# The warm-up products of an encoder layer's opening read a constant, and are 16 instead of 14

## The chip, the cores and the metric

The kernel runs on one core of a Trainium2 chip. The time is that of the device in microseconds (us), from the program's start to its end; a kernel is run several times, and the median counts. A profile shows one further execution: when every instruction began on each engine, how long it took and what ended the idle time before it. The engines are PE (TensorE, matrix products; PEld is its loading of weights), DVE (VectorE), ACT (ScalarE), POOL (GpSimd) and SP (SyncE, which here sends off transfers). "PEq", "SPq" are the instruction sequencers of an engine. Times in the profile count from the first instruction of the execution.

## The reference

One layer of a streaming encoder in float32, for a sequence of 256 frames of width 2048.

```python
h = rms_norm(x, attn_norm)
x = x + hybrid_mixer(h, w_in, b_forget, q_norm, k_norm, out_norm_fox, out_norm_sb, w_out)
h = rms_norm(x, ffn_norm)
x = x + conv_ffn(h, w_up, conv_w, conv_b, w_down)
```

`hybrid_mixer` multiplies h by `w_in` (2048 x 6152), runs eight heads of forgetting attention and eight heads of stick-breaking attention, normalises the two groups apart, and multiplies by `w_out` (2048 x 2048). `conv_ffn` multiplies by `w_up` (2048 x 11264), applies a causal convolution of width 3 over time, gates one half with the SiLU of the other, and multiplies by `w_down` (5632 x 2048).

## The kernel before

Every product of the reference is made of three products of halves. A float32 weight is loaded (`load`, L197, tile `w_raw`), rounded on ScalarE to a coarser type (`w_hi`, L207), and VectorE makes the rest (`w_lo` = raw - hi, L208). TensorE then adds hi x hi, lo x hi and hi x lo in an accumulator (`in_three`, L221, with the tokens as rows; `from_features`, L249, with the features as rows). Activations are split in the same way: `transposed_split` (L133) transposes four blocks of x on TensorE (`ps_x`, L138), and writes the high part on ScalarE (L143) and the low part on VectorE (L146) into `hT`.

The stages, in the program's order:

- **Opening** (L385 to L474). x, the gains and the first weights of `w_in` are loaded in small pieces. While they travel, `keep_busy` (L379) gives TensorE products whose result `idle` nobody reads: 14 before the gains are transposed (`columns`, L126), and 4 more after the first four transposes of x. Their operand is `zeros`, a tile of 128 x 256 bf16 in the pool `at`, written by VectorE (L371). Then the first piece of weights is split, and the first products into `acc` run (L428).
- **Projections and heads** (L481 to L772): the rest of `w_in`, then the sixteen heads.
- **Output projection** (L781 to L807): for each of two groups of heads and each of four blocks c of 512 columns, `acc` is formed with `w_out` (L229), and VectorE adds it to x (L803). In the second group, ScalarE sums the squares of the new x (`junk`, L155), and the transposes of the new x for the FFN wait for a later step (`next_rows`, L776).
- **Factors of the tokens** (`token_factors`, L157): the sums of squares are reduced (L161), and a reciprocal root is taken: two steps on ScalarE (L112, L113), the others on VectorE (L111 to L117); two diagonal tiles `dg` follow (L166).
- **FFN** (L814 to the end): a list of steps. Each has a load, sent off six steps ahead, a split, two steps ahead, and its products; the first column block of `w_up` is `pu` (L254 high, L260 low), in two pieces of 8 x 128 rows.

Tiles live in pools, stacked in memory in the order in which they are opened. The attention stage opens `at` (L289), `tmp`, `wraw` (three buffers of 8192 bytes in each partition), `whi` and `wlo` (two each), and closes them at its end; the FFN opens its own `wlo2`, `whi2` (three each), `wraw2` (four) and `wsum` in the memory that has come free (L814 to L817). The scheduler makes the first instruction that writes to a pool wait for the last readers of what lay in that memory before. In the opening and the FFN the order on each engine is as written; from the end of the opening to the FFN only TensorE's is, and the scheduler chooses the others' by priority and by what it expects to be free.

Of the kernel before, what the change touches and what calls it, by code (L numbers as in the profile page):

```python
# [14 lines left out]
P = 128  # L15
D = 2048
S = 256
# [28 lines left out]
def hybrid_layer(  # L46
# [19 lines left out]
    nc = tc.nc  # L66
    act, dve = nc.scalar, nc.vector
# [10 lines left out]
    def f32(t):  # L78
        return t.bitcast(F32)
# [10 lines left out]
    def load_x(k, n):  # L90
        nc.sync.dma_start(x2[:, :, k * P : (k + n) * P], xp[:, :, k * P : (k + n) * P])
# [34 lines left out]
    def columns(dst, rows, n):  # L126
        pp = psb.tile([P, 512], F32, name="pp", tag="t")
        nc.tensor.transpose(pp[:, :n], rows, ident[:n, :n])
        dve.tensor_copy(dst, pp[:, :n])
# [3 lines left out]
    def transposed_split(k, g, n=2):  # L133

        ps = psb.tile([P, 2, S], F32, name="ps_x", tag="t")
        for j in range(n):
            for t in range(NT):
                nc.tensor.transpose(  # L138
                    ps[:, j, t * P : (t + 1) * P], xt[t][:, (k + j) * P : (k + j + 1) * P], ident
                )  # L140
        for j in range(n):
            i = k + j
            act.activation(hT[:, i, 0, :], ps[:, j, :], AF.Identity, scale=g[:, i : i + 1])  # L143
        for j in range(n):
            i = k + j
            dve.scalar_tensor_tensor(  # L146
                hT[:, i, 1, :], ps[:, j, :], g[:, i : i + 1], f32(hT[:, i, 0, :]),
                op0=ALU.mult, op1=ALU.subtract,
            )

    def sums_of_squares(ss, c, tiles=range(NT)):

        for t in tiles:
            junk = late.tile([P, 512], F32, name="junk", tag="raw", bufs=4)
            act.activation(junk, xt[t][:, c * 512 : (c + 1) * 512], AF.Square, accum_out=ss[:, t, c : c + 1])  # L155
# [62 lines left out]
    def rows_of(w, k0, n, c0, cols):  # L218
        return w[k0 * P : (k0 + n) * P, c0 : c0 + cols].rearrange("(k p) c -> p k c", p=P)
# [14 lines left out]
    def of_half(h, part, t):  # L234
        return h[:, part, t * P : (t + 1) * P]
# [51 lines left out]
    with ExitStack() as actx:  # L287

        at = actx.enter_context(tc.tile_pool(name="at", bufs=1))  # L289
# [77 lines left out]

        zeros = at.tile([P, S], mybir.dt.bfloat16, name="zeros")  # L370
        dve.memset(zeros, 0.0)  # L371
        nc.gpsimd.memset(ident, 0.0)
        nc.gpsimd.affine_select(
            ident, ident, pattern=[[-1, P]], base=0, channel_multiplier=1,
# [2 lines left out]
        idle = pss.tile([P, S], F32, name="idle", tag="s")  # L377

        def keep_busy(n):  # L379
            for _ in range(n):  # L380
                nc.tensor.matmul(idle, zeros[:, :P], zeros, start=True, stop=True)

        ss1 = const.tile([P, NT, 4], F32, name="ss1")

        def opening():  # L385

            acc = psa.tile([P, NT, 512], F32, name="acc", tag="acc")
            pairs = [[(0, 1), (1, 1)]] + [[(0, 2)]] * 7
            raws, parts = [], []

            def load_w(c, which=None, queue=nc.sync):

                if c == len(raws):
                    raw = wraw.tile([P, 2048], F32, name="w_raw", tag="w_raw")
                    raws.extend([raw[:, :1024], raw[:, 1024:]])
                for i, n in [(which, 1)] if which is not None else [(0, 2)]:
                    queue.dma_start(
                        raws[c][:, i * 512 : (i + n) * 512].rearrange("p (a b) -> p a b", a=n),
                        rows_of(wi, 2 * c + i, n, 0, 512),
                    )  # L400

            def split_w(c):
                hi = whi.tile([P, 2048], F32R, name="w_hi", tag="w_hi")
                lo = wlo.tile([P, 2048], F32R, name="w_lo", tag="w_lo")
                parts.append([t[:, :1024].rearrange("p (a b) -> p a b", a=2) for t in (hi, lo)])
                for i, n in pairs[c]:
                    cols = slice(i * 512, (i + n) * 512)
                    if c == i == 0:
                        dve.tensor_copy(hi[:, cols], raws[c][:, cols])
                        for k in range(2):  # L410
                            transposed_split(k, ga, 1)
                    elif c == 1:
                        for j in range(2):
                            half = slice(512 * j, 512 * (j + 1))
                            dve.tensor_copy(hi[:, half], raws[c][:, half])
                        transposed_split(2, ga)
                    else:
                        act.copy(hi[:, cols], raws[c][:, cols])
                    dve.tensor_tensor(
                        lo[:, cols], raws[c][:, cols], f32(hi[:, cols]), op=ALU.subtract  # L420
                    )

            def multiply(c, i, n, high):
                hi, lo = (p[:, i : i + n] for p in parts[c])
                order = [(j, l, hi) for j in range(n) for l in range(2)] if high else [(j, 0, lo) for j in range(n)]
                for m, (j, l, r) in enumerate(order):
                    for t in range(NT):
                        nc.tensor.matmul(  # L428
                            acc[:, t, :], of_half(hT[:, 2 * c + i + j], l, t), r[:, j, :],
                            start=high and c == i == m == 0, stop=not high and c == 7 and m == n - 1,  # L430
                        )

            load_x(0, 2)
            nc.scalar.dma_start(prow[:KT, :], attn_norm[0].rearrange("(n p) -> n p", p=P))
            act.preload_act_table_set("natural_log_exp_and_others")
            load_w(0, 0)
            load_w(0, 1, nc.scalar)
            load_x(2, 2)
            load_w(1, 0, nc.scalar)
            load_w(1, 1)  # L440
            load_x(4, 2)
            load_w(2)
            load_x(6, 2)
            load_w(3)
            load_x(8, 4)
            load_w(4)
            load_x(12, 4)
            load_w(5)
            keep_busy(14)
            columns(ga, prow[:KT, :], KT)  # L450
            split_w(0)
            keep_busy(4)

            def behind(c):
                if c:
                    transposed_split(2 * c + 2, ga)
                split_w(c + 1)

            multiply(0, 0, 1, True)
            multiply(0, 1, 1, True)  # L460
            behind(0)
            sums_of_squares(ss1, 0, [0])
            multiply(0, 0, 1, False)
            multiply(0, 1, 1, False)
            for c in range(1, 8):
                if c < 7:
                    behind(c)
                sums_of_squares(ss1, c // 2, [c % 2])
                if c == 2:
                    load_w(6)  # L470
                    load_w(7)
                multiply(c, 0, 2, True)
                multiply(c, 0, 2, False)
            return acc  # L474

        with tc.high_priority(offset=AHEAD), tc.manual_schedule(
            engines={mybir.EngineType.PE, mybir.EngineType.DVE, mybir.EngineType.Activation, mybir.EngineType.SP}
        ):
            acc_q0 = opening()
# [301 lines left out]
        for group in range(2):  # L781
# [3 lines left out]
            for c in range(4):  # L785
# [7 lines left out]
                if c == 0:  # L793
                    pg = psb.tile([P, NT], F32, name="pg", tag="t")
                    for t in range(NT):
                        nc.tensor.matmul(
                            pg[:, t : t + 1], ssq[group][:, t * P : (t + 1) * P], ones[:, 0:1],
                            start=t == 0, stop=t == NT - 1,
# [376 lines left out]
```

## Time and profile before

| What | us |
|---|---|
| median of three runs (lowest to highest) | 1103.35 (1103.25 to 1103.62) |
| the profiled execution's own time | 1103.81 |
| its span, from the first to the last instruction | 1102.0 |
| TensorE busy in the span | 1096.5 |
| VectorE busy | 877.7 |
| ScalarE busy | 701.9 |
| GpSimd busy | 44.4 |

The span is the time that the engines' instructions cover; the execution's own time has some start and end beside it (1.8 us here). The mean granted clock of TensorE over the span is 1.000 of full speed. The profile is read by groups (the page), by what each engine waited for, by a timeline of one stretch, and by the chain of waits, which is followed back from the last instruction. A row such as "6.02 0.43 DVE L409 CAST ... [1.56 <-DMA ...]" says: began at 6.02 us, took 0.43 us, on VectorE, line 409; VectorE had been idle for 1.56 us, until a transfer landed.

### The profile page before, as it was taken

What the parts mean: (1) busy time and instruction counts of PE and PEld (TensorE: products, weight loads), DVE (VectorE), ACT (ScalarE), POOL (GpSimd) and SP (SyncE); (2) the same over time, 40 slices, a digit from 0 to 9 for tenths busy, and PEclk for the clock granted to TensorE, in tenths of its full rate; (3) what the DMA queues carried; (4) which work ended last, traced back from release to release, by engine and by line L of the source; (5) the groups of instructions that cost most, each with busy time, mean ns of one, the idle gap of its engine ahead of it and who ended that gap; (6) DMA issues with size and microseconds to landing.
All of it is one profiled execution on the core that took longest, in us unless ns stands there. A gap on an engine that the chain in (4) does not pass through costs nothing.

```text
span 1102.0 us, 14826 instructions
## 1 busy us (share of the span) xinstructions
PE 1096.5 (99%) x5868; PEld 951.2 (86%) x5868; DVE 877.7 (80%) x941; ACT 701.9 (64%) x879; POOL 44.4 (4%) x46
## 2 busy tenths in 40 slices
PE   9999999999999999999999999999999999999998
PEld 7998888888888888888888888888888888888887
DVE  5655777975775677689889988889798889889896
ACT  6544556664653566677767776767676777677753
POOL 0000000000000000000000010100000010100010
PEclk9999999999999999999999999999999999999999
DMA  8776654576545396558989597986979689997985
GB/s 288 171 244 230 188 156 153 153 231 197 184 161 186 112 317 196 181 191 209 288 223 312 191 234 264 261 269 177 315 209 303 217 218 282 241 266 198 322 208 177
DMA packets 179407, 245.89 MB, mean 223 GB/s; under 512 B 4432, under 2 KB 119018, under 8 KB 179082
## 3 DMA queue, kind: packets, MB, share of 16 engines
q1 hardware_dynamic: 162458, 209.67, 58.6%
q0 software_dynamic: 16560, 34.75, 16.8%
q8 instruction: 46, 0.75, 0.3%
q10 hardware_dynamic: 320, 0.53, 0.1%
q14 instruction: 23, 0.19, 0.0%
HBM read 242.82 MB, written 2.11 MB: 222 GB/s over the span
## 4 chain that ended last, share of the span: by engine, by line
PE 99%; DMA 0%; DVE 0%; SPq 0%; issue 0%
PE pu L254 34%; PE acc L229 22%; PE pu L260 18%; PE bank_a L229 10%; PE bank_b L229 5%; PE bank_c L229 2%; PE acc L428 2%; PE acc L1053 1%; PE ps_x L138 1%; PE ps_o L593 1%; PE bank_a L1053 1%; PE ps_p L607 0%; DMA w_raw<-in_w_in_dram 0%; PE ps_o L594 0%; PE ps_h L307 0%; PE ps_s L522 0%
## 5 line engine op out<-in xcount | busy, mean ns | idle before, releaser
L208 DVE TENSOR_TENSOR w_lo<-w_raw,w_hi 128x2048 fp32r<-128x2048 f32 (+1 forms) x196 | 439.6, 2246 | 129.5 <-ACT w_hi L207 128.6
L207 ACT CAST w_hi<-w_raw 128x2048 fp32r<-128x2048 f32 (+1 forms) x196 | 367.3, 1877 | 235.9 <-PE acc L229 66.6
L254 PE MATMUL pu<-hT,w_hi 128*128 128x512 f32 x1664 | 394.0, 390 | 0.0
L254 PEld LDWEIGHTS pu<-hT,w_hi 128*128 128x128 f32 x1664 | 310.3, 188 | 63.2
L260 PEld LDWEIGHTS pu<-hT,w_lo 128*128 128x128 f32 x1664 | 211.9, 191 | 7.0
L260 PE MATMUL pu<-hT,w_lo 128*128 128x256 f32 x1664 | 215.1, 283 | 0.0
L229 PE MATMUL acc<-w_hi,hT 128*128 128x512 f32 (+1 forms) x576 | 124.5, 368 | 0.0
L229 PEld LDWEIGHTS acc<-w_hi,hT 128*128 128x128 f32 x576 | 101.5, 188 | 14.3
L207 ACT CAST w_hi<-w_sum 128x2048 fp32r<-128x2048 f32 x30 | 57.3, 1909 | 44.2 <-PE pu L254 36.6
L208 DVE TENSOR_TENSOR w_lo<-w_sum,w_hi 128x2048 fp32r<-128x2048 f32 x30 | 68.7, 2290 | 20.8 <-ACT w_hi L207 20.7
L870 ACT ACTIVATE tap<-up,ccol 128x256 f32<-128x256 f32 x176 | 74.6, 495 | 0.0
L229 PE MATMUL acc<-w_lo,hT 128*128 128x512 f32 (+1 forms) x288 | 64.6, 366 | 0.0
L229 PEld LDWEIGHTS acc<-w_lo,hT 128*128 128x128 f32 x288 | 51.6, 188 | 7.5
L975 POOL DMA_DIRECT2D w_sum<-in_w_down_dram x20 | 25.7, 1284 | 797.7 <-DVE w_lo L208 786.1
L229 PE MATMUL acc<-w_hi,oT 128*128 128x512 f32 x192 | 46.0, 392 | 0.0
L229 PEld LDWEIGHTS acc<-w_hi,oT 128*128 128x128 f32 x192 | 35.7, 188 | 7.3
L229 PE MATMUL bank_a<-w_hi,g 128*128 128x512 f32 x160 | 40.0, 392 | 0.0
L229 PE MATMUL bank_b<-w_hi,s 128*128 128x512 f32 x160 | 40.0, 392 | 0.0
L229 PE MATMUL bank_a<-w_hi,s 128*128 128x512 f32 x160 | 40.0, 392 | 0.0
L229 PEld LDWEIGHTS bank_b<-w_hi,s 128*128 128x128 f32 x160 | 28.9, 189 | 5.2
L229 PEld LDWEIGHTS bank_a<-w_hi,g 128*128 128x128 f32 x160 | 28.8, 189 | 5.3
L229 PEld LDWEIGHTS bank_a<-w_hi,s 128*128 128x128 f32 x160 | 28.9, 189 | 5.2
(211 smaller groups left out, 1068.7 us busy)
## 6 DMA issues: line engine op xcount, KB each, us to landing
w_raw<-in_w_up_dram SPq DMA_DIRECT2D x88, 1024.0 KB, 7.5
w_raw<-in_w_down_dram SPq DMA_DIRECT2D x44, 1024.0 KB, 6.4
w_raw<-in_w_in_dram SPq DMA_DIRECT2D x36, 1024.0 KB, 5.4
w_sum<-in_w_down_dram POOLq DMA_DIRECT2D x20, 1024.0 KB, 9.9
w_raw<-in_w_out_dram SPq DMA_DIRECT2D x16, 1024.0 KB, 5.1
w_raw<-in_w_down_dram POOLq DMA_DIRECT2D x10, 1024.0 KB, 14.9
w_raw<-in_w_in_dram SPq DMA_DIRECT2D x12, 688.0 KB, 4.2
w_raw<-in_w_in_dram SPq DMA_DIRECT2D x6, 512.0 KB, 6.8
```

The lines of the kernel that those rows point to most:

```text
L138: nc.tensor.transpose(ps[:, j, t * P : (t + 1) * P], xt[t][:, (k + j) * P : (k + j + 1) * P], ident)
L207: act.copy(hi[:, :n], raw[:, :n])
L208: dve.tensor_tensor(lo[:, :n], raw[:, :n], f32(hi[:, :n]), op=ALU.subtract)
L229: nc.tensor.matmul(o, lhs(i, l, t), r[:, i, :], start=starts and j == 0, stop=stops and j == 3 * n - 1, skip_group_check=more,)
L254: nc.tensor.matmul(acc[:, j, :], hi[:, i, j * P : (j + 1) * P], hT[:, k].rearrange("p a b -> p (a b)"), start=k == 0, stop=low_first and k ...
L260: nc.tensor.matmul(acc[:, j, S:], lo[:, i, j * P : (j + 1) * P], hT[:, k, 0, :], start=False, stop=not low_first and k == KT - 1,)
L428: nc.tensor.matmul(acc[:, t, :], of_half(hT[:, 2 * c + i + j], l, t), r[:, j, :], start=high and c == i == m == 0, stop=not high and c == ...
L593: nc.tensor.matmul(po, v[j][:, hs], wp[:, k], start=i == 0, stop=False)
L870: act.activation(taps[w][:, j, :], u[:, j, w : w + S], AF.Copy, scale=ccol[:, w, f : f + 1])
L975: nc.gpsimd.dma_start(mem[into][:, : nk * 512].rearrange("p (a b) -> p a b", a=nk), src, accum_op=ALU.add)
L1053: nc.tensor.matmul(o, of_half(g, l, t), r[:, i, c0 : c0 + cols], start=kh == 0 and j == 0, stop=kh == n - 1 and j == 11,)
```

## The change

The tile `zeros` and its memset go. `keep_busy` reads `some`, a view of a constant that the program's preamble writes on GpSimd before any kernel instruction (one bf16 1.0 in each partition, read again and again), and the first call makes 16 products.

```diff
-        zeros = at.tile([P, S], mybir.dt.bfloat16, name="zeros")
-        dve.memset(zeros, 0.0)
+        some = nc.const_aps.tensor(1.0, [P, S], mybir.dt.bfloat16)
...
         def keep_busy(n):
             for _ in range(n):
-                nc.tensor.matmul(idle, zeros[:, :P], zeros, start=True, stop=True)
+                nc.tensor.matmul(idle, some[:, :P], some, start=True, stop=True)
...
-            keep_busy(14)
+            keep_busy(16)
```

The pool `at` is 512 bytes smaller in each partition by this, and the scheduler's order differs from before at three places. Behind the change the lines of the kernel have numbers smaller by one.

VectorE at the start of the program, before and after; what an instruction waits for stands in brackets:

```order
L1170 UNCONDITIONAL_BRANCH [waits barrier_Pool_Activation_PE_DVE_SP_release]
L371 MEMSET zeros 128x128
L129 COPY ga<-pp 128x16 [waits PE_49]
L409 COPY w_hi<-w_raw 128x512 [waits DMAHW2_49]
L146 TENSOR_SCALAR hT<-ps_x,ga,hT 128x256 [waits Activation_49] x2
```

```order
L1169 UNCONDITIONAL_BRANCH [waits barrier_Pool_Activation_PE_DVE_SP_release]
L825 MEMSET up_3577 128x2x2
L825 MEMSET up_3578 128x2x2
L129 COPY ga<-pp 128x16 [waits PE_49]
L408 COPY w_hi<-w_raw 128x512 [waits DMAHW2_49]
```

The memset of `zeros` is gone, and two small memsets of the FFN (`up`, before at the border of the stages) stand in its place.

SP at the border between the output projection and the FFN, as a difference (`DMAHW` and `DMASW` are queues of transfers, the other names engines):

```order
 L200 DMA w_raw<-in_w_out_dram 128x4x512 [waits DMAHW5_49,DVE_49]
-L200 DMA w_raw<-in_w_up_dram 128x8x256 [waits DMAHW6_49,DMAHW0_49,DMAHW7_49,DMASW3_49,DVE_49]
+L200 DMA w_raw<-in_w_up_dram 128x8x256 [waits DMAHW0_49,DMAHW6_49,DMASW3_49,DMAHW7_49,DVE_49,PE_49]
 L200 DMA w_raw<-in_w_up_dram 128x8x256 x3
 L200 DMA w_raw<-in_w_up_dram 128x8x256 [waits DMAHW1_49,DVE_49]
 L200 DMA w_raw<-in_w_up_dram 128x8x256 [waits DMAHW2_49,DVE_49]
```

The first load of `w_up` has a wait for PE that it did not have; the three behind it have none of their own, as before.

ScalarE at the same border, before and after (`w_hi` casts of FFN weights, L207; squares, L155; reciprocal root, L112 and L113; `hT`, L143, the last quarter of x):

```order
L143 ACTIVATE hT<-ps_x,pcol 128x256 [waits PE_49]
L143 ACTIVATE hT<-ps_x,pcol 128x256
L207 COPY w_hi<-w_raw 128x2048 [waits DMASW4_49,DMASW5_49,DMASW2_49,DMAHW1_49,Activation_49,Pool_49]
L207 COPY w_hi<-w_raw 128x2048 [waits DMAHW2_49]
L155 ACTIVATE junk,ss_2828<-x_2945 128x512 [waits DVE_49] x2
L207 COPY w_hi<-w_raw 128x2048 [waits DMAHW3_49]
L112 ACTIVATE rs_y<-rs_a 128x2 [waits DVE_49]
L113 ACTIVATE rs_y<-rs_y 128x2 [waits Activation_49]
```

```order
L143 ACTIVATE hT<-ps_x,pcol 128x256 [waits PE_49]
L143 ACTIVATE hT<-ps_x,pcol 128x256
L155 ACTIVATE junk,ss_2828<-x_2945 128x512 [waits DVE_49,Activation_49] x2
L112 ACTIVATE rs_y<-rs_a 128x2 [waits DVE_49]
L113 ACTIVATE rs_y<-rs_y 128x2 [waits Activation_49]
L207 COPY w_hi<-w_raw 128x2048 [waits DMASW4_49,DMASW5_49,DMASW2_49,DMAHW1_49,PE_49,Pool_49]
L207 COPY w_hi<-w_raw 128x2048 [waits DMAHW2_49]
L207 COPY w_hi<-w_raw 128x2048 [waits DMAHW3_49]
```

The three casts have moved behind the squares and the reciprocal root, and the first of them waits for PE. On VectorE the three `w_lo` of these weights have moved in the same way, behind the reciprocal root and the two `dg`. TensorE's order is the same but for the two added products and the second call of `columns`, which stands two products earlier.

## The prediction

> **What bounds the kernel now.** I read first the busy shares and the chain that ended last (page, parts 1 and 4), then everything that TensorE waited for, then the two places where the order of instructions changes: the opening and the border between attention and the feed-forward part (FFN).
>
> ```profile
> PE 1096.5 (99%) x5868; PEld 951.2 (86%) x5868; DVE 877.7 (80%) x941; ACT 701.9 (64%) x879; POOL 44.4 (4%) x46
> PE 99%; DMA 0%; DVE 0%; SPq 0%; issue 0%
> PE idle L381 <- DVE zeros L371: 1.1, 1, 1.1
> PE acc L428 <- DVE w_hi L409: 1.1, 1, 1.1
> PE ps_x L138 <- DMA x<-in_x_dram: 0.2, 1, 0.2
> ```
>
> TensorE sets the end: 1096.5 of the span of 1102.0 us. The last three rows are its whole list of waits (engine, line, releaser: us, times, longest), and all three lie in the opening. So two things follow. A faster opening can return at most 1.1 + 1.1 + 0.2 = 2.4 us. And after it TensorE has no waiting left that could swallow a delay: whatever holds it at any later place is added to the end one for one.
>
> The timeline of the opening (start, duration, engine, line; in brackets the idle time before and its releaser), and one row of the chain of waits (the DMA):
>
> ```profile
> 0.83 0.17 DVE L371 MEMSET zeros<- 128x128 uint32 x1 [0.83 <-PEq L1160]
> 1.06 3.04 PE L381 MATMUL idle<-zeros 128*128 128x256 bf16 x14 [1.06 <-DVE zeros L371]
> 1.23 4.77 DMA w_raw<-in_w_in_dram
> 4.03 0.22 PE L128 MATMUL pp<-cs,prow 16*128 16x16 f32 x1
> 4.29 0.17 DVE L129 COPY ga<-pp 128x16 f32<-128x16 f32 x1 [3.29 <-PE pp L128]
> 4.45 0.66 PE L138 MATMUL ps_x<-cs,x 128*128 128x128 f32 x4 [0.20 <-DMA x<-in_x_dram]
> 4.93 0.84 ACT L143 ACTIVATE hT<-ps_x,ga 128x256 fp32r<-128x256 f32 x2 [2.42 <-PE ps_x L138]
> 6.02 0.43 DVE L409 CAST w_hi<-w_raw 128x512 fp32r<-128x512 f32 x1 [1.56 <-DMA w_raw<-in_w_in_dram]
> 6.59 2.06 PE L428 MATMUL acc<-w_hi,hT 128*128 128x512 f32 x8 [1.05 <-DVE w_hi L409]
> ```
>
> The first real products start at 6.59 because the first weights land at 1.23 + 4.77 = 6.00. Of what the change touches there, nothing sends that transfer off earlier.
>
> The timeline at the border, and six rows of the chain of waits (the last six; start, duration, what):
>
> ```profile
> 383.96 2.28 DVE L208 TENSOR_TENSOR w_lo<-w_raw,w_hi 128x2048 fp32r<-128x2048 f32 x1
> 386.28 13.29 SPq L200 DMA_DIRECT2D w_raw<-in_w_up_dram  x6
> 389.33 3.89 PE L229 MATMUL acc<-w_hi,hT 128*128 128x512 f32 x16
> 391.42 1.91 ACT L207 CAST w_hi<-w_raw 128x2048 fp32r<-128x2048 f32 x1 [0.67 <-DMA w_raw<-in_w_up_dram]
> 393.36 2.29 DVE L208 TENSOR_TENSOR w_lo<-w_raw,w_hi 128x2048 fp32r<-128x2048 f32 x1 [1.65 <-ACT w_hi L207]
> 394.34 1.92 ACT L207 CAST w_hi<-w_raw 128x2048 fp32r<-128x2048 f32 x1 [1.02 <-DMA w_raw<-in_w_up_dram]
> 395.57 1.40 DVE L803 SCALAR_TENSOR_TENSOR x<-acc,rg,x 128x512 f32<-128x512 f32 x2
> 397.54 0.19 ACT L155 ACTIVATION_READ_ACCUMULATOR junk<-x 128x1 f32 x1
> 399.09 0.15 DVE L161 TENSOR_REDUCE ssum<-ss 128x2 f32<-128x8 f32 x1
> 399.71 0.20 ACT L113 ACTIVATE rs_y<-rs_y 128x2 f32<-128x2 f32 x1
> 389.58 5.46 PE acc L229 x24
> 395.03 1.81 PE pu L254 x8
> 396.85 0.95 PE pu L260 x8
> 397.80 1.84 PE pu L254 x8
> 399.64 0.95 PE pu L260 x8
> 400.59 0.88 PE ps_x L138 x8
> ```
>
> Here the first FFN weights are asked for at 386.28, the moment the last w_lo of the attention stage is made (383.96 + 2.28 = 386.24), are split at 391.42 to 393.33, and so are ready 1.7 us before TensorE leaves the last attention product at 395.03. The border is seamless, by a margin of only 1.7 us.
>
> **The change, part by part.**
>
> *The opening.* The wait for the memset goes: TensorE can begin at about 0.85, when VectorE could begin its memset, and not at 1.06. Two products more, at 3.04 / 14 = 0.217 us each, make 16 x 0.217 = 3.47 us and end near 4.32, against 1.06 + 3.04 = 4.10 now. The transposition of the gains behind them (L128, 4.03) comes some 0.2 later, ga some 0.2 later, the four transposes (4.45) and hT (4.93 to 5.77) at most 0.3 later, 6.07. VectorE uses hT only after its cast of the weights, at 6.02 + 0.43 = 6.45. So 0.4 us of cover is left, under the transfer that lands at 6.00: cost and gain 0. Without that cover it would cost 0.3. The two small memsets of `up` that VectorE now does first take the place of the memset of zeros, in front of 3.29 us of idle time (row of 4.29): 0. The transposition of the parameters (L128, second call) goes two products earlier in TensorE's order and the product gq one place up on VectorE: no work is added, 0.
>
> *The border: the load.* The tile zeros took 512 bytes in each partition. Without it every tile of the attention stage that lies behind it moves down by 512 bytes. The FFN's four raw buffers end at byte 154,656 of a partition; the attention stage's w_hi buffers began at 154,912 and now begin at 154,400. The two overlap by 256 bytes, and the order of SP shows what comes of it: the first load of w_up now waits for PE too. The value it waits for is that of the sixteenth product with the last w_hi of the attention stage, which ends at 389.33 + 3.89 = 393.22 and not 386.24. All later loads on SP are queued behind it. From issue to cast the first load took 391.42 - 386.28 = 5.14 us. That puts the cast at 393.25 + 5.14 = 398.4.
>
> *The border: the order on ScalarE and VectorE.* The same overlap puts ScalarE's casts of the first three FFN weights behind the squares (L155) and the two steps of the reciprocal root (L112, L113), which need the last attention product. When would ScalarE be free? The product ends at 395.04; VectorE's two additions take 1.40 (row of 395.57), to 396.5; the last square's accumulator is read 397.73 - 396.97 = 0.76 after them, 397.2; from the reduction to the end of L113 it takes 399.91 - 399.09 = 0.82: 398.1. This is 0.3 before the load lands, so of the two causes the load decides, and the order alone would give a cast at 398.1 even with the old load. Either suffices for nearly the whole stall.
>
> *The sum.* Cast 398.4 + 1.91 = 400.3. TensorE begins 0.14 later, as it did after the cast at 6.45 (6.59 - 6.45): 400.4. It has stood since 395.04: 5.4 us. Its first eight products end 1.81 later, at 402.2; the next eight need w_lo, 2.29 after the cast, 402.6, and the same 0.1 to begin: 0.5 us more. Then the weights are ahead again: the second load is cast 394.34 - 391.42 = 2.9 after the first, at 401.3, its w_lo is ready at 401.3 + 1.92 + 2.29 = 405.5, and TensorE asks for it after its transposes, at 400.59 + 0.88 + 5.9 = 407.4. The transposes themselves now stand behind a wait for eight products; their order is unchanged. Total 5.4 + 0.5 = 5.9, and with a tenth for the first product's slow start 6.0 us. The profiled execution took 1103.81 us around its span of 1102.0; the span becomes 1108.0. The median of the runs, 1103.35, becomes 1109.4. Bounds of this sum: if transfers after an idle queue land faster, ScalarE's order still holds the cast to 398.1, so 5.6 at least less 0.3 for the starts: 5.3. If the first load needs half a microsecond longer, 6.5.
>
> **The rivals.**
>
> *The clock of TensorE falls in the gap.* The new gap of 5.4 us is longer than any in this trace after the start (1.05 us is the longest). The opening shows what a product costs at first: 0.217 us for 256 columns, against 0.95 / 8 = 0.119 in the row of 396.85, and this for less than 4.95 - 1.06 = 3.9 us. If it were so again, up to 3.9 us at half pace lose 1.9 us, of which 0.4 hide under the wait for w_lo: 0 to 1.5 more, 1109.7 to 1110.9. For it: the gap's length. Against: no row shows how long a gap it takes.
> The Trainium skill, "TensorE: Matmul & The Clock Gate", Part 1, has the clock halved after a whole idle window of about 3.4 us, the windows running free of the kernel; by that rule a gap of 5.4 us holds a whole window in some runs and not in others, which speaks against this change beyond the stall itself; no row of this trace can show it at the border.
>
> *The FFN stays starved.* The loads behind the first are late as well, and if the second landed over 1.9 us (407.4 - 405.5) later than reckoned, TensorE would stop again: 1 to 3 us more, 1110.9 to 1112.4. Against it is the row of the border by slices of 0.8 us:
>
> ```profile
> GB/s 0 0 0 0 0 0 0 0 0 111 360 385 379 348 349 347 348 349 347 349 347 348 349 348 347 349 356 337 346 351 348 346 289 250 335 348 348 348 348 348
> ```
>
> At 350 GB/s a load of 1.05 MB takes 3.0 us, and TensorE needs 1.81 + 0.95 + 1.84 + 0.95 = 5.6 us for each: it catches up 2.6 us with every load.
>
> *Not slower: the opening pays and the border does not.* The border costs nothing if TensorE's last attention products run ahead of the load's wait, which takes two things: a wait that is over by 386.3, and casts that do not sit behind the squares. Then only the opening counts, between 0 and its 2.4 us: 1101.0 to 1103.4. It decides if both orders are harmless; the 1.7 us of margin against 7.0 us of delay (393.22 - 386.24) leave little room.
>
> *It does what it says and no more* (the wait for the memset is gone, the rest hidden): 1103.3, by the same two conditions.
>
> **How the numbers follow.** The stall at full clock has 0.50 and gives 1109.4 (its own range 1108.7 to 1109.9); the fallen clock 0.33; starvation 0.11; the opening paying 0.03; no effect 0.03. The range 1108.3 to 1111.5 holds the first, all of the second, and a third of the third case, with a little below for shorter starts. Within 0.2% means within 2.2 us, about what a measurement can tell: faster 0.03, same 0.03, slower 0.94.
>
> **What would show it.** In the profile after: TensorE's list of waits has a new row, pu (L254) waiting for ScalarE's w_hi, about 5.4 us once, and one for w_lo (L260) of about 0.5; the first SP row of w_up stands near 393.2 and not 386.3; ScalarE's first FFN cast begins at 398 to 399, behind L113; the opening still has its first real product at 6.6. Products of 512 columns at 0.43 us right after the gap would show the fallen clock. The prediction is wrong if the first w_up load is issued by 387, if the cast starts before 396, or if the gap is there and the end is not later by it.

## The result and the profile after

The changed kernel takes 1110.56 us (median of six runs, 1110.18 to 1111.87), the kernel before 1103.3: a ratio of 1.0067, with a 95% interval of 1.0054 to 1.008. It is 7.3 us slower, by an edit that was made 390 us ahead of the place where the time is lost. The profiled execution took 1110.36, its span is 1108.6. Of all runs below one is left out, an execution of the kernel with 224 unused bytes (e4) that took 1566.71 us at a mean clock of 0.654.

TensorE's list of waits (engine, line, releaser: us in total, times, longest) now has these three rows:

```profile
PE pu L254 <- ACT w_hi L207: 5.3, 1, 5.3
PE idle L380 <- PEq L1159: 0.8, 1, 0.8
PE acc L427 <- DVE w_hi L408: 0.6, 1, 0.6
```

The opening waits for 1.4 us and no longer for 2.4. A new wait of 5.3 us stands at the first product of `pu`, and the mean granted clock over the span is 0.998, not 1.000.

The opening in the timeline after:

```profile
0.78 3.33 PE L380 MATMUL idle<-const-bfloat16-1.0 128*128 128x256 bf16 x16 [0.78 <-PEq L1159]
4.04 0.23 PE L128 MATMUL pp<-cs,prow 16*128 16x16 f32 x1
5.44 0.43 DVE L408 CAST w_hi<-w_raw 128x512 fp32r<-128x512 f32 x1 [0.96 <-DMA w_raw<-in_w_in_dram]
6.01 2.08 PE L427 MATMUL acc<-w_hi,hT 128*128 128x512 f32 x8 [0.59 <-DVE w_hi L408]
```

The warm-up products start 0.28 us earlier, the gains are transposed at 4.04 as before (4.03), and the first weights' cast still ends a wait for their transfer. This transfer landed 0.58 us earlier in this execution (5.44 against 6.02); whether the change did that is a question for the experiments.

The border between the output projection and the FFN, timeline after:

```profile
388.77 3.89 PE L229 MATMUL acc<-w_hi,hT 128*128 128x512 f32 x16
392.50 1.98 PE L229 MATMUL acc<-w_lo,hT 128*128 128x512 f32 x8
392.69 12.69 SPq L200 DMA_DIRECT2D w_raw<-in_w_up_dram  x6
394.51 1.41 DVE L802 SCALAR_TENSOR_TENSOR x<-acc,rg,x 128x512 f32<-128x512 f32 x2 [3.36 <-PE acc L229]
397.40 0.20 ACT L113 ACTIVATE rs_y<-rs_y 128x2 f32<-128x2 f32 x1
397.82 1.90 ACT L207 CAST w_hi<-w_raw 128x2048 fp32r<-128x2048 f32 x1 [0.22 <-DMA w_raw<-in_w_up_dram]
399.78 3.63 PE L254 MATMUL pu<-hT,w_hi 128*128 128x512 f32 x8 [5.31 <-ACT w_hi L207]
```

The load is issued as the sixteen products with the last w_hi of the attention stage end (388.77 + 3.89 = 392.66), where before it left 6.9 us ahead of that end. ScalarE was free from 397.60, after L113, and waited 0.22 for the load. Then the first eight products of `pu` took 3.63 us, and 1.81 before.

The chain of waits gives the border's price in two rows, from one set of transposes of x to the next:

```profile
388.14 0.87 PE ps_x L138 x8
392.69 5.04 DMA w_raw<-in_w_up_dram
397.82 1.91 ACT w_hi L207
399.78 3.63 PE pu L254 x8
407.15 0.87 PE ps_x L138 x8
```

The border takes 407.15 - 388.14 = 19.01 us; before it took 400.59 - 388.70 = 11.89. The difference is 7.12 us. The first transposes before, and TensorE's last row in the chain, before and after:

```profile
388.70 0.87 PE ps_x L138 x8
1093.18 5.60 PE bank_a L1053 x36
1099.72 5.60 PE bank_a L1052 x36
```

From the second transposes to the end of that last row it is 1093.18 + 5.60 - 400.59 = 698.19 us before and 1099.72 + 5.60 - 407.15 = 698.17 after. So the whole span is accounted for: -0.56 ahead of the border, +7.12 in it, -0.02 behind it, together +6.54, against spans that differ by 6.6.

Why the first products were slow shows by stretches of 1 us, after (the length, then the busy us of PE, PEld, DVE, ACT and POOL with their instructions, then TensorE's granted clock, the share of the transfers and their GB/s):

```profile
398.00:399.00 1.00, 0.00 (x0) 0.00 (x0) 0.81 (x4) 1.00 (x1) 0.00 (x0) 1.00 1.09 348
399.00:400.00 1.00, 0.22 (x1) 0.23 (x2) 0.24 (x1) 0.72 (x1) 0.00 (x0) 0.83 1.10 348
400.00:401.00 1.00, 1.00 (x3) 0.81 (x4) 1.00 (x1) 0.24 (x1) 0.00 (x0) 0.50 1.09 348
403.00:404.00 1.00, 1.00 (x9) 0.95 (x8) 1.00 (x1) 0.23 (x1) 0.00 (x0) 0.96 1.08 345
```

The clock went to half at 399.67 (a mean of 0.83 over 399 to 400), as the weights were all but ready, and came back at 403.08.

### The profile page after: what moved, and what is told of

It reads as the page before. It is cut to its first block, busy times and chain, and to the rows that moved or that the text cites. A ratio compares the mean times of both kernels' runs of the same rounds, so it can differ in the third digit from the quotient of the medians.

```text
span 1108.6 us, 14829 instructions
## 1 busy us (share of the span) xinstructions
PE 1098.6 (99%) x5870; PEld 952.5 (86%) x5870; DVE 878.5 (79%) x940; ACT 702.8 (63%) x879; POOL 44.4 (4%) x46
## 4 chain that ended last, share of the span: by engine, by line
PE 99%; DMA 1%; ACT 0%; DVE 0%; SPq 0%; issue 0%; ACTq 0%
PE pu L254 34%; PE acc L229 22%; PE pu L260 18%; PE bank_a L229 10%; PE bank_b L229 5%; PE bank_c L229 2%; PE acc L427 2%; PE acc L1052 1%; PE ps_x L138 1%; PE ps_o L592 1%; PE bank_a L1052 1%; PE ps_p L606 0%; DMA w_raw<-in_w_up_dram 0%; DMA w_raw<-in_w_in_dram 0%; PE ps_o L593 0%; PE ps_h L307 0%
## 5 line engine op out<-in xcount | busy, mean ns | idle before, releaser
L207 ACT CAST w_hi<-w_raw 128x2048 fp32r<-128x2048 f32 (+1 forms) x196 | 367.8, 1879 | 236.7 <-PE acc L229 67.4
L207 ACT CAST w_hi<-w_sum 128x2048 fp32r<-128x2048 f32 x30 | 57.3, 1911 | 42.9 <-PE pu L254 36.8
L208 DVE TENSOR_TENSOR w_lo<-w_sum,w_hi 128x2048 fp32r<-128x2048 f32 x30 | 68.7, 2290 | 19.5 <-ACT w_hi L207 19.4
```

Source lines behind the costliest of these rows:

```text
L207: act.copy(hi[:, :n], raw[:, :n])
L208: dve.tensor_tensor(lo[:, :n], raw[:, :n], f32(hi[:, :n]), op=ALU.subtract)
```

## The experiments

The theory: the 512 bytes of the tile `zeros` are the cause. Without them two pools overlap, the first FFN load waits for the pool's last reader, the scheduler puts the casts behind the squares and the root, TensorE stands for 5.3 us, and the clock falls in the gap. The rivals: the constant or the two products more cost the time; any shift of the tiles does; the load alone or the order alone matters; the slow products after the gap are not the clock's.

**The layout put back, the rest of the change kept** (e1).

```diff
         some = nc.const_aps.tensor(1.0, [P, S], mybir.dt.bfloat16)
+        at.tile([P, 256], mybir.dt.bfloat16, name="pad")
```

> The changed kernel with an unused tile of 512 bytes a partition in the pool `at`, so that all tiles lie where they lay before the change; 16 products that read the constant stay. Theory (the overlap of the FFN's raw buffers with the attention stage's w_hi is the whole loss): no PE wait at the first w_up load, that load near 386, TensorE without a wait for pu, 1102.7 to 1103.4 us. Where in this range tells whether the opening's 0.6 us earlier start is the change's doing (1102.7) or the execution's (1103.3). Rival (reading the constant, or two products more, costs the time): 1110 us or so, as the changed kernel.

Measured: 1103.42 us (11 runs), a ratio of 0.9999 to the kernel before (0.999 to 1.0008). The chain of waits shows the old border, 400.17 - 388.27 = 11.90:

```profile
388.27 0.87 PE ps_x L138 x8
394.61 1.81 PE pu L254 x8
400.17 0.87 PE ps_x L138 x8
```

An unused tile takes all of the loss away. The products of the constant cost nothing and gain nothing that these runs can tell; the interval is some 1 us to each side.

**The layout alone** (e2): the kernel before, its 14 products and its memset, with `zeros` in a pool behind w_hi.

```diff
-        zeros = at.tile([P, S], mybir.dt.bfloat16, name="zeros")
+        zeros = late.tile([P, S], mybir.dt.bfloat16, name="zeros")
```

> The kernel before, 14 products that read the tile zeros and VectorE's memset, but zeros lies in the pool `late`, which is opened behind w_hi, so that w_hi lies 512 bytes lower, as after the change. Theory (overlap): the first w_up load waits for PE, at about 393, pu waits some 5.3 us for its first cast, the clock falls, 1110.2 to 1111.9 us; 1110.9 in the middle if the opening gains nothing here. Rival (the constant or the products cost the time): 1103.3 us.

Measured: 1111.39 us (5 runs), ratio 1.0069 (1.0056 to 1.0081). TensorE's waits:

```profile
PE pu L254 <- ACT w_hi L207: 5.5, 1, 5.5
PE idle L381 <- DVE zeros L371: 1.1, 1, 1.1
```

The loss is there without the constant and without the added products. Its border takes 20.09 us, 1.1 more than that of the change: its wait is 0.2 longer, and in this execution the clock stayed at half for 6.8 us, twice as long.

**The number of products** (e8): 14 products of the constant, with the old layout.

```diff
+        at.tile([P, 256], mybir.dt.bfloat16, name="pad")
...
-            keep_busy(16)
+            keep_busy(14)
```

> As the kernel with 512 unused bytes, but with 14 products of the constant at first and not 16. Theory (the opening waits for the first weights' transfer): the same as with 16, within 0.3 us, 1102.7 to 1103.4 us, first real product when the first weights have landed. Rival (the two products more keep the clock up and bring the opening forward): 0.3 to 1 us slower than with 16.

Measured: 1103.39 us (11 runs), ratio 1.0000 (0.9991 to 1.0008): the same as with 16. Its first real product starts at 6.34. Over all profiles of this study that start lies between 5.88 and 6.59, with `zeros` (6.59 before, 6.08 in e2) as with the constant (6.01 after, 6.46 and 6.51 in two others). So nothing ties the 0.58 us of the profile after to the change; executions of one kind differ by as much.

**Where the loss begins** (e3, e4): 256 and 224 unused bytes. With 256, w_hi begins exactly where the FFN's raw buffers end; with 224, 32 bytes overlap.

```diff
         some = nc.const_aps.tensor(1.0, [P, S], mybir.dt.bfloat16)
+        at.tile([P, 128], mybir.dt.bfloat16, name="pad")
...
+        at.tile([P, 112], mybir.dt.bfloat16, name="pad")
```

> The changed kernel with 256 unused bytes a partition in `at`: w_hi begins at byte 154,656, exactly where the FFN's raw buffers end. Theory (overlap): nothing overlaps, 1102.7 to 1103.4 us, no wait for pu. Rival (any shift of the tiles, by their place alone, slows the border or the engines): between 1103.4 and 1110.5, about half of the loss for half of the shift.

> The changed kernel with 224 unused bytes a partition in `at`: w_hi begins at byte 154,624, and 32 bytes overlap. Theory (overlap): the full loss, as with 256 bytes, 1110.2 to 1111.9 us, pu waiting 5.3 us. Rival (a loss that grows with the shift or with the bytes in common): under 1107 us, near to the kernel with 256 unused bytes.

Measured: 1103.45 us with 256 (10 runs; ratio 1.0, 0.999 to 1.0009), 1114.25 with 224 (three runs; ratio 1.0098, 1.0082 to 1.0113). The step is where it was expected, and no loss grows with the shift. With 256, three of the ten runs lie 1 to 3 us above the others, the profiled one (1106.32) among them; its border takes 400.09 - 388.20 = 11.89, as before, and its added time lies behind the border, with 1.8 us of waits in the FFN. The kernel with 224 is 2.4 us above its range. Its border costs what it should: the same wait of 5.3 us, and 411.93 - 391.98 = 19.95 us between the transposes. The excess lies ahead of it: the transposes begin 3.8 us later than in e2 (391.98 against 388.22), without a wait of TensorE.

**The excess** (e9, e10): 480 unused bytes overlap nothing, but put w_hi as many bytes beyond a multiple of 256 from hT as 224 do; 192 overlap by 64 bytes.

```diff
         some = nc.const_aps.tensor(1.0, [P, S], mybir.dt.bfloat16)
+        at.tile([P, 240], mybir.dt.bfloat16, name="pad")
...
+        at.tile([P, 96], mybir.dt.bfloat16, name="pad")
```

> The changed kernel with 480 unused bytes a partition in `at`: nothing overlaps at the border, but the attention stage's tiles lie 32 bytes off their old places, so that w_hi begins at a multiple of 64 bytes while hT does not (before, both lay 32 bytes behind one). With 224 unused bytes the products of the attention stage that read w_hi and hT took 232 to 234 ns in the median and not 227, in all 3.8 us up to the border. Theory (operands of a product that lie differently towards 64 bytes cost it 2 to 3%): 1106.6 to 1107.6 us with no wait for pu. Rival (the 3.8 us were a disturbance of that execution, or came from the border): 1102.9 to 1103.7 us.

> The changed kernel with 192 unused bytes a partition in `at`: 64 bytes overlap, and all tiles lie towards 64 bytes as before. Theory (any overlap costs the whole stall; the excess of the 32-byte overlap was the operands' place): 1110.2 to 1111.9 us, as the changed kernel with its 256 bytes in common. Rival (a small overlap costs more, whatever the place): 1113.5 us or more.

Measured: 1107.3 us with 480 (ratio 1.0035, 1.0021 to 1.0049), as the theory had it, with a border of 404.08 - 392.05 = 12.03. With 192 it was 1114.71 (1.0101, 1.0086 to 1.0117): the theory's range was missed, and the rival's number was met. The rival's mechanism was not. The chain of e10:

```profile
391.39 0.87 PE ps_x L138 x8
396.02 5.07 DMA w_raw<-in_w_up_dram
403.14 3.78 PE pu L254 x8
411.63 0.44 PE ps_x L138 x4
```

Its border takes 411.63 - 391.39 = 20.24 us, as e2's with the clock low for as long (20.09), and it reaches the border 3.3 us later than the changed kernel (391.39 against 388.14). The overlap again cost the same; what failed was the reckoning with 64 bytes. The groups of products between 30 and 380 us, each shape apart (busy us, mean ns of one), first of the changed kernel, then of e9, show what is slower (`oT` is the output of the heads):

```profile
L229 PE MATMUL acc<-w_hi,hT 128*128 128x512 f32 x365 | 87.8, 393 | 0.0
L254 PE MATMUL pu<-hT,w_hi 128*128 128x512 f32 x256 | 60.8, 391 | 0.0
L229 PE MATMUL acc<-w_hi,oT 128*128 128x512 f32 x176 | 42.2, 392 | 0.0
```

```profile
L229 PE MATMUL acc<-w_hi,hT 128*128 128x512 f32 x352 | 86.4, 398 | 0.0
L254 PE MATMUL pu<-hT,w_hi 128*128 128x512 f32 x256 | 62.0, 396 | 0.0
L229 PE MATMUL acc<-w_hi,oT 128*128 128x512 f32 x176 | 42.2, 392 | 0.0
```

The products of 512 columns that read w_hi and hT take 5 ns more each. Those that read w_hi and `oT` don't: `oT` lies behind w_hi and moved with it, so w_hi's own place is not what costs. From hT (byte 37,408, as the sizes of the tiles ahead of it add up) to the attention stage's first w_hi the distance is a multiple of 256 bytes in the kernels before and after and in e3, and leaves 224 in e4 and e9 and 192 in e10. A multiple of 64 is thus not enough (e10). Whether 128 or 256 is what counts, these kernels don't tell.

**All tiles moved together** (e12): the old layout, with 32 bytes more in the pool `const`, so that every large tile begins at a multiple of 64.

```diff
     bf = const.tile([P, NH], F32, name="bf")
+    const.tile([P, 8], F32, name="pad32")
...
+        at.tile([P, 256], mybir.dt.bfloat16, name="pad")
```

> The changed kernel with 512 unused bytes in `at` and 32 more in `const`: every tile behind it begins at a multiple of 64 bytes, so all operands of a product lie alike towards 64 bytes, and the transposes' identity, which lay at a multiple of 64 before, now lies like x. Theory (only a difference between a product's operands counts): 1103.4 us, or up to 1 us less if the transposes gain. Rival (a multiple of 64 is slow in itself): 1107 us or more.

Measured: 1103.51 us (11 runs; ratio 1.0003, 0.9994 to 1.0011). A move of all tiles by 32 bytes costs nothing, so the distance between the two operands counts here and not a place towards 64 bytes; the transposes gained nothing.

**The order without the late load** (e6): the old layout, and a copy of two columns that ties the first cast to the root.

```diff
+    roots, behind_root = [], []
...
         act.activation(y, y, AF.Exp, scale=-0.5)
+        roots[:] = [y]
...
         n = a * b
+        if behind_root:
+            act.copy(hi[:, :2], behind_root.pop())
         act.copy(hi[:, :n], raw[:, :n])
...
+        at.tile([P, 256], mybir.dt.bfloat16, name="pad")
...
     rstd2, dg2 = token_factors(ss2, 2)
+    behind_root[:] = roots
```

> The changed kernel with 512 unused bytes in `at` (no overlap, first w_up load at about 386), but a copy of two columns from the reciprocal root into the first FFN w_hi, ahead of its cast, which puts ScalarE's and VectorE's order at the border as the changed kernel has it: casts behind squares and root. Theory (load and order each suffice alone): the cast starts 3.3 to 3.5 us after TensorE's last attention product, pu waits 5.2 to 5.5 us, 1109.8 to 1111.5 us. Rival (the late load alone matters): 1102.7 to 1103.6 us.

Measured: 1112.14 us (4 runs; ratio 1.0078, 1.0064 to 1.0092). Its border in the timeline:

```profile
385.56 5.21 SPq L203 DMA_DIRECT2D w_raw<-in_w_up_dram  x4
392.35 1.98 PE L234 MATMUL acc<-w_lo,hT 128*128 128x512 f32 x8
397.25 0.20 ACT L115 ACTIVATE rs_y<-rs_y 128x2 f32<-128x2 f32 x1
397.75 5.50 ACT L212 CAST w_hi<-w_raw 128x2048 fp32r<-128x2048 f32 x3
399.75 3.75 PE L259 MATMUL pu<-hT,w_hi 128*128 128x512 f32 x8 [5.43 <-issue]
```

The weights are asked for at 385.56 and three of them wait in memory, for the casts run one behind the other without a pause. Still TensorE stands for 5.43 us. The order alone makes the whole gap. The time is above the range by 0.6; the profiled execution, the slowest of the four, took 2.4 us more behind the border than that of the changed kernel, with a wait of 1.5 for an addition in the FFN (`bank_a`, from VectorE). Such a wait appeared in the profiles of e3 (1.0) and e7 (0.9) too, and not in that of the changed kernel. Its cause was not looked for.

**The late load without the order** (e7): the changed layout, the factors of the tokens formed one step later.

```diff
-    rstd2, dg2 = token_factors(ss2, 2)
...
+            if n == 0:
+                rstd2, dg2 = token_factors(ss2, 2)
             if n == 1:
                 tokens.append(in_every_partition(dg2, 2, const))
```

> The changed kernel with its overlap, but the factors of the tokens are formed later, behind the first FFN splits, so that ScalarE's casts of the first three FFN weights stand ahead of the root (the squares stay ahead of them). Theory (each suffices alone): the load is issued at about 393 and the cast starts 5.1 us later, as in the changed kernel: pu waits 5.2 to 5.4 us, 1110.0 to 1111.9 us. Rival (the order alone matters): 1102.7 to 1104 us.

Measured: 1111.17 us (4 runs; ratio 1.0067, 1.0051 to 1.0082). The first cast, ahead of the root now, waits for the transfer:

```profile
392.79 12.79 SPq L200 DMA_DIRECT2D w_raw<-in_w_up_dram  x6
398.02 1.90 ACT L207 CAST w_hi<-w_raw 128x2048 fp32r<-128x2048 f32 x1 [1.19 <-DMA w_raw<-in_w_up_dram]
399.98 3.61 PE L254 MATMUL pu<-hT,w_hi 128*128 128x512 f32 x8 [5.40 <-ACT w_hi L207]
```

The load alone makes the whole gap as well. Whoever undid only one of the two would have found no gain.

**The clock** (e5, e11): 20 and 44 more products of the constant in the gap.

```diff
+            if n == 0:
+                more = psf.tile([P, S], F32, name="more", tag="a")
+                for _ in range(20):
+                    nc.tensor.matmul(more, some[:, :P], some, start=True, stop=True)
             at(0, 3)
```

> The changed kernel with 20 more products of the constant between TensorE's last attention product and the first of pu, where it stands idle for 5.3 us. At full clock they take 20 x 0.107 = 2.2 us and leave about 3.1 us of idle time. Theory (the gap costs 5.3 us, and the clock that falls in it the rest): the clock stays up, the first eight pu products take 1.8 us and not 3.6, then 0.4 us of wait for w_lo: 1.3 to 1.5 us less than the changed kernel, 1109.0 to 1109.4 us. Rival (the slow products after the gap are the price of a first use of the new weights, or of w_lo, not of the clock): 1110.5 us.

> The changed kernel with 44 more products of the constant in TensorE's gap: 44 x 0.107 = 4.7 of 5.3 us are filled. Theory (the gap's own price is 5.3 us, what is above it comes from the clock): the clock stays at 1.000 in every run, the time is 1109.0 to 1109.7 us, and the runs lie closer together than those of the changed kernel. Rival (the excess over 5.3 us is not the clock's): 1110.5 us, as the changed kernel.

With 20 products the median is 1110.67 us (5 runs; ratio 1.0063, 1.005 to 1.0075), which is the rival's number. The five runs differ, though. The profiled one kept a clock of 1.000 and took 1109.55; three had a mean clock of 0.998, as the changed kernel has, and took 1110.36 to 1110.79; the fifth had 0.999 and took 1111.5, which a fall of the clock does not explain. The profiled one:

```profile
394.42 2.41 PE L1123 MATMUL more<-const-bfloat16-1.0 128*128 128x256 bf16 x20
399.99 2.11 PE L254 MATMUL pu<-hT,w_hi 128*128 128x512 f32 x8 [3.16 <-ACT w_hi L207]
402.31 1.21 PE L260 MATMUL pu<-hT,w_lo 128*128 128x256 f32 x8 [0.22 <-DVE w_lo L208]
```

The eight products are fast here, and TensorE waits 0.22 us for w_lo. The border takes 406.32 - 388.24 = 18.08 us. With 44 products the clock was 1.000 in four runs and 0.999 in one, the border took 406.60 - 388.61 = 17.99, and the time was 1110.11 us (1109.59 to 1110.57; ratio 1.006, 1.0048 to 1.0073). That is 0.4 above the range; its profiled execution, at 1110.57 the slowest, waited 0.5 us for `bank_a` in the FFN. So the clock's part is plain in the border of the profiled executions: 18.0 or 18.1 us with the clock up, 19.0 with 3.4 us of half clock, 20.1 with 6.8 (19.5 in e6, where 2.7 of the 6.8 lie in the gap). The medians alone don't show it: the ratios' intervals of e5 and e11 overlap that of the changed kernel.

No version was found that beats the kernel before; e1, e3, e8 and e12 equal it.

## Why the prediction was right, point by point

- *The opening: 0.* Right. e1 and e8 measure it with the border put back: ratios of 0.9999 and 1.0000. Its cover, the first weights' transfer, was there in the profile after (0.96 us of VectorE's idle time before its cast). Two of its signs came out otherwise: the sixteen products took 3.33 us and not 3.47, so the gains were not later (4.04), and the first real product stood at 6.01 and not at 6.6.
- *The load waits for the sixteenth product.* Right: issued at 392.69, 0.03 after that product's end; 5.13 us from issue to cast, against the 5.14 reckoned.
- *ScalarE free 0.3 before the load lands; either cause suffices.* Right: 0.22 in the profile, and shown apart by e6 and e7.
- *The gap: 5.4.* Measured 5.31.
- *The wait for w_lo: 0.5, and the sum 6.0.* In the profile after no such wait stands, for the slow products fill it. At full clock the wait was 0.22 (e5); from the first product of `pu` to the first with w_lo it was 402.31 - 399.99 = 2.32 us, against 1.81 + 0.5 reckoned, and the border grew by 18.08 - 11.89 = 6.2 (e5) and 6.1 (e11).
- *The weights are ahead again.* Right: the rest takes 698.19 us before and 698.17 after, so the rival of a starved FFN falls.
- *The clock.* This is the step that was mis-sized. The case at full clock had 0.50 and was named as the likeliest, the fallen clock 0.33. It fell in all six runs of the changed kernel, as their mean clocks of 0.997 or 0.998 say. The sign named for it was there: 3.63 / 8 = 0.45 us a product behind the gap. Its price, 0 to 1.5 us reckoned, was 7.12 - 6.1 = 1.0 for the short fall and 20.09 - 11.89 - 6.1 = 2.1 for the long one (0.2 of it the longer wait of e2). The prediction reckoned with 3.9 us of half clock at most, and did not have the 6.8. So the median came out 1.2 us above the 1109.4, within the range and in the rival's own stretch of 1109.7 to 1110.9.

The Trainium skill, "TensorE: Matmul & The Clock Gate", Part 1, has the clock fall after a whole idle window of some 3.4 us. The trace after agrees, with 5.2 us of standing before the fall. e6 doesn't: TensorE stopped at 392.35 + 1.98 = 394.33, and the clock was at half from 397.0.

```profile
394.00:395.00 1.00, 0.32 (x2) 0.00 (x0) 0.64 (x1) 0.00 (x0) 0.00 (x0) 1.00 1.11 352
396.00:397.00 1.00, 0.00 (x0) 0.00 (x0) 0.35 (x4) 0.58 (x2) 0.00 (x0) 1.00 1.09 347
397.00:398.00 1.00, 0.00 (x0) 0.00 (x0) 0.45 (x3) 0.85 (x4) 0.00 (x0) 0.51 1.09 346
```

In these rows of e6 2.7 us of idle time were enough, and in three runs of e5 (0.998) so, it seems, were 3.2. A reckoning by a whole idle window takes the fall for too rare.

## What to carry to other kernels

A tile that goes away moves all tiles behind it in its stage, and where the next stage's memory ends within the old one's by a few bytes, its first load may wait for quite another pool: compare the waits and the order of the first load behind each border, and keep the place with an unused tile when they differ. Where one event makes both a transfer and the order of an engine late, undo both before judging either. A gap on TensorE like those here (3.2 to 5.5 us) is to be priced with a fall of its clock, some 1 to 2 us more.

## What the runs showed of the hardware that was not expected

- Products of 512 columns whose operands, hT and w_hi, lie apart by 192 or 224 bytes more than a multiple of 256 take 2 to 5 ns more of some 391 to 393 (e9 and e10, each shape apart), 3.9 us in all (e9: 1107.3 against 1103.39), without any wait in the profile. Those of 344 columns take the same (319 and 320), and those of 256 columns, with w_lo, take 3 ns less (283 and 280, e9).
- The clock can fall after 2.7 us of standing (e6). It then came back after 3.4 us where TensorE was busy almost from the fall on (after: fell 399.67, busy from 399.78; e7 likewise, 0.15 later), and after 6.8 us where it began 1.0 to 2.7 us later (e10, e4, e6, and e2: products from 400.0, clock at half from 398.6 to 405.4):

```profile
398.00:399.00 1.00, 0.00 (x0) 0.00 (x0) 0.88 (x5) 0.93 (x1) 0.00 (x0) 0.79 1.09 347
404.00:405.00 1.00, 1.00 (x7) 1.00 (x6) 1.00 (x1) 0.99 (x1) 0.00 (x0) 0.50 1.09 347
405.00:406.00 1.00, 1.00 (x6) 0.91 (x6) 0.28 (x2) 0.91 (x1) 0.00 (x0) 0.79 1.10 349
```
